# Attention step of a hybrid encoder: the transposes of a block ahead of the scores of a later one, and another rate for the convolution taps

## The chip, the cores and the metric

The kernel runs on one core of a Trainium2 chip, in one launch. The metric is device time in microseconds (us), the median of several runs. The core's engines are TensorE (PE for its matmuls, PEld for its weight loads), VectorE (DVE), ScalarE (ACT), GpSimd (POOL) and SyncE (SP), which here only issues DMAs.

## The reference

One layer of a streaming encoder on a prompt of 1024 frames and 32 frames of a running stream, with 16 heads of 64 and a model width of 1024. Everything starts from one combined projection of the normalised input.

```python
h = rmsnorm(x, norm_g)
cols = lambda a, w: h @ w_in[:, a:a + w]
q = rmsnorm(cols(OFF_Q, ...).reshape(B, T, N_HEADS, HEAD_DIM), q_g) * (HEAD_DIM ** -0.5)
k = rmsnorm(cols(OFF_K, ...), k_g); v = cols(OFF_V, ...)
logf = jax.nn.log_sigmoid(cols(OFF_F, N_HEADS) + b_f)
u = cols(OFF_UA, CONV_WIDTH) * jax.nn.sigmoid(cols(OFF_UB, CONV_WIDTH))
...
s = jnp.einsum('bqhd,bkhd->bhqk', q, k)
s = jnp.where(mask, s + (cq - ck), -inf)          # c = cumsum(logf)
o = jnp.einsum('bhqk,bkhd->bqhd', jax.nn.softmax(s), v)
conv = causal_dwconv(u_ext, w_dw, b_dw)           # 31 taps for each channel
...
ya = (o * jax.nn.silu(ga)) @ w_pa
yb = (jax.nn.silu(layernorm(conv, ln_g, ln_b)) * jax.nn.silu(gb)) @ w_pb
m = jax.nn.sigmoid(ma) * ya + jax.nn.sigmoid(mb) * yb
return x + m @ w_out
```

Two parts of it meet in the change: the causal attention of the prompt, and the depthwise convolution with the LayerNorm over its channels.

## The kernel before, in words

The kernel works with channels on the partitions and frames along the free dimension, and goes through the projections (up to 566 us), the attention (566 to 1045 us) and the output projections. A product in full precision is made of three products of rounded parts (wh, wl for the weight, xh, xl for the input), which line 183 issues. Within a stretch marked as manually scheduled, PE, DVE and ACT, and in the attention SP too, take their instructions in the order in which the program lists them. POOL's order is the scheduler's. An engine does one instruction after another, so one that waits holds up all that is listed behind it.

**The attention.** The list `seq` has, for each of the 16 heads, eight `Block`s (128 queries each, block i with (i + 1) x 128 keys) and in four places a `Sample`, which handles four heads of the running stream: 132 items. The loop at L1244 goes through it, and its step n deals with several items in different stages of their work:

- `scores` (L1110) of item n + 3, through `start`: two matmuls (L1121, L1122) for each bank of up to 512 keys into a psS tile; then on DVE the causal mask is added (L1124) and the maximum taken (L1126).
- `turn` (L1141) of item n: POOL clears a strip (L1146); PE transposes P block by block (L1153) into tiles of psT, which has two banks. The first four transposed blocks are copied out by ACT, the rest (blocks 4 to 7 of a head have some) by DVE (both L1156).
- `soft` (L1129) of item n + 3: the exponential on ACT (L1133), with the sum of each row.
- `norm` (L1136) of item n + 2: the reciprocal on DVE (L1138), the product of P with it on POOL (L1139).
- `fill`, four beats in two halves: a beat is one eighth of a third of a further projection (gates, three matmuls at L183); their results leave through ACT (L944) to DRAM.
- `values` (L1158) of item n - 2, for the last block of a head: 40 matmuls (L1172) into two psT tiles, their copy by ACT (L1176) and sum by DVE (L1177), and for an odd head the product with a gate (L1179) that a DMA brought (L1161).
- one piece of the LayerNorm over channels (L1206 to L1230), once the sums that it needs are there. Its first four pieces are empty; then come six with two matmuls each (L1202), then twelve with small operations of ACT and DVE.

In the first three blocks of head 8 `fill` does nothing (L1258).

**What rides on the beats.** `beat` (L199) counts time in the program's order. It issues the pieces of weight preparation that are due (`prep`: square and maximum, then wh on ACT at L138, wl on DVE at L141), the delayed pieces (`late`), and the convolution's taps. A tap (L371) is one DVE operation over 1086 columns with two tensors read. Taps wait in a list and are dealt by a credit: every beat adds `pace["rate"]`, and while the credit is not negative, the next item is issued and its price taken off, 1 for a tap and 0.1 for the first tap of a channel block, which runs on ACT (L368).

```python
if taps or chores:
    pace["credit"] += pace["rate"]
while pace["credit"] >= 0 and (taps or chores):
    ...
        cost = taps.pop(0)() or 1.0
    pace["credit"] -= cost
```

The rate in the attention is `R_A` (L34, set at L999). Behind the taps of a channel block come its sums (L334, L339); the last block's sums, nine and thirteen beats later (L355, L351), make the LayerNorm ready.

Of the kernel before, what the change touches and what calls it, by code (L numbers as in the profile page):

```python
# [30 lines left out]
LNO = ((0,), (1, 2), (3,), (4, 5), (6,), (7,), ())  # L31
LNEXP = "natural_log_exp_and_others"
NFILL = 22
R_U, R_V, R_QK, R_G, R_A = 0.21, 0.18, 0.165, 0.23, 0.2  # L34
NWARM = 34
HT = TT // 2
HC = HT // 2
# [16 lines left out]
def build(tc, xT, xt, wv, wf, ckT, cv, clT, stT, vec, cst, yT, kT, vO, lfO, cpT, csT):  # L54
# [968 lines left out]
    def fill(n):  # L1023
        for _ in range(n):
            next(flow, None)
# [163 lines left out]
    def start(b):  # L1189
        if getattr(b, "i", 1) == 0:  # L1190
            h = b.head
            if h.h % 2 == 0:
                h.ot = heads[h.h + 1].ot = ap.tile([128, T], F32, name="ot", tag="ot", bufs=2)
        b.scores()

    def pending(b):
        return isinstance(b, Sample) or b.i % 2
# [40 lines left out]
    for n in range(3):  # L1238
# [3 lines left out]
            seq[n - 1].norm()  # L1242
        fill((8, 4, 0)[n])
    for n, b in enumerate(seq):  # L1244
        if n + 3 < len(seq):
            start(seq[n + 3])
        if n + 9 < len(seq) and getattr(seq[n + 9], "i", 1) == 0:
            seq[n + 9].head.load()
        if n + 6 < len(seq) and isinstance(seq[n + 6], Sample):
            seq[n + 6].load()  # L1250
        if getattr(b, "i", 0) == 3 and b.head.h + 1 < H:
            heads[b.head.h + 1].load_v()
        b.turn()
        if n + 3 < len(seq):
            seq[n + 3].soft()
        if n + 2 < len(seq):
            seq[n + 2].norm()
        some = 2 if isinstance(b, Sample) or b.i > 2 or b.head.h != 8 else 0  # L1258
        fill(some)
        if n >= 2 and pending(seq[n - 2]):  # L1260
            seq[n - 2].values()
        fill(some)
        if n >= 3 and isinstance(seq[n - 3], Sample):
            seq[n - 3].finish()
        if "ready" in sides:
            next(ln, None)
# [402 lines left out]
```

## Time and profile before

| | us |
|---|---|
| median of three runs | 1346.9 (1346.65 to 1347.09) |
| the profiled execution | 1345.89 |
| its span, first to last instruction | 1344.1 |
| the attention within it | 566 to 1045 |
| PE busy / DVE busy over the span | 1312.6 / 990.4 |

The profile shows one execution. Times are microseconds from the span's first instruction; a row of a group of instructions gives line, engine, operation, what it writes and reads, count, then the busy time, the mean in ns, and the idle time of the engine just ahead of them with what ended it. In a row of waits, "PE ptr L1153 <- DVE pt L1156: 7.8, 8, 1.7" says that PE's instruction of line 1153 waited for DVE's of line 1156 for 7.8 us in eight places, 1.7 at most. A row of the timeline gives start, duration, engine, line, operation, and in brackets the engine's idle time before it. The ends of matmuls are modelled, and those that follow each other closely overlap.

### The profile page before, as it was taken

What the parts mean: (1) busy time and instruction counts of PE and PEld (TensorE: products, weight loads), DVE (VectorE), ACT (ScalarE), POOL (GpSimd) and SP (SyncE); (2) the same over time, 40 slices, a digit from 0 to 9 for tenths busy, and PEclk for the clock granted to TensorE, in tenths of its full rate; (3) what the DMA queues carried; (4) which work ended last, traced back from release to release, by engine and by line L of the source; (5) the groups of instructions that cost most, each with busy time, mean ns of one, the idle gap of its engine ahead of it and who ended that gap; (6) DMA issues with size and microseconds to landing.
All of it is one profiled execution on the core that took longest, in us unless ns stands there. A gap on an engine that the chain in (4) does not pass through costs nothing.

```text
span 1344.1 us, 24837 instructions
## 1 busy us (share of the span) xinstructions
PE 1312.6 (98%) x9383; PEld 1003.1 (75%) x9383; DVE 990.4 (74%) x1532; ACT 719.0 (53%) x1362; POOL 505.8 (38%) x548
## 2 busy tenths in 40 slices
PE   8999999999999999999889998999999999999999
PEld 5687876666666666667567766777776699999998
DVE  6797879888999997987778866655554489166664
ACT  6644555757676743455555555655555566233320
POOL 2001124547484820243433442222222158255562
PEclk8999999999999999999999999999999999999999
DMA  6343233425352463535644643565452698544462
GB/s 251 98 140 104 93 112 118 139 82 187 95 180 87 162 166 109 160 90 155 165 109 123 186 132 99 147 179 132 131 152 54 240 313 262 176 128 146 142 190 69
DMA packets 113496, 194.97 MB, mean 145 GB/s; under 512 B 34080, under 2 KB 80032, under 8 KB 113376
## 3 DMA queue, kind: packets, MB, share of 16 engines
q1 hardware_dynamic: 113232, 193.31, 46.9%
q8 instruction: 74, 1.21, 0.4%
q14 instruction: 46, 0.38, 0.1%
q10 hardware_dynamic: 144, 0.07, 0.0%
HBM read 127.68 MB, written 65.64 MB: 144 GB/s over the span
## 4 chain that ended last, share of the span: by engine, by line
PE 82%; DVE 9%; ACT 3%; issue 2%; DMA 2%; SPq 1%; POOL 0%; DVEq 0%; ACTq 0%; POOLq 0%
PE pj L183 56%; PE pjv L761 6%; PE pj L1501 6%; PE po L1172 4%; PE ptr L1153 3%; DVE nm L1126 2%; DVE wl L141 2%; DVE y L371 2%; PE psS L1122 2%; PE psS L1121 2%; DMA ga<-s_ga 2%; ACT wh L138 1%; DVE psS L1124 1%; DMA s_q<-qh 1%; PE warm L477 1%
## 5 line engine op out<-in xcount | busy, mean ns | idle before, releaser
L183 PE MATMUL pj<-xh,wh 128*128 128x352 f16 (+2 forms) x1536 | 481.6, 314 | 2.3 <-ACT wh L138 1.4
L183 PE MATMUL pj<-xh,wl 128*128 128x352 f16 (+2 forms) x1536 | 481.2, 313 | 0.7 <-DVE wl L141 0.6
L183 PE MATMUL pj<-xl,wh 128*128 128x352 f16 (+2 forms) x1536 | 480.9, 313 | 0.5 <-DVE xl L579 0.4
L183 PEld LDWEIGHTS <-wh 128*128 128x128 f16 x3072 | 301.5, 98 | 162.1 <-issue 7.1
L371 DVE SCALAR_TENSOR_TENSOR y<-u,vec_t,y 128x1086 f32<-128x1086 f32 x240 | 346.8, 1446 | 12.0 <-ACT y L368 8.9
L1139 POOL TENSOR_SCALAR P<-P,nm 128x128 f32<-128x128 f32 (+7 forms) x128 | 129.9, 1015 | 279.9 <-DVE nm L1138 229.8
L183 PEld LDWEIGHTS <-wl 128*128 128x128 f16 x1536 | 150.5, 98 | 72.0 <-DVE wl L141 1.6
L141 DVE SCALAR_TENSOR_TENSOR wl<-raw,sc,wh 128x384 f16<-128x384 f32 (+1 forms) x192 | 128.2, 693 | 48.3 <-ACT wh L138 48.3
L1133 ACT ACTIVATE P<-psS,nm 128x128 f32<-128x128 f32 (+7 forms) x128 | 95.1, 743 | 113.3 <-DVE nm L1138 70.9
L1126 DVE TENSOR_REDUCE nm<-psS 128x1 f32<-128x128 f32 (+7 forms) x128 | 97.0, 758 | 12.5
L1153 PE MATMUL ptr<-ident,P 128*128 128x128 f32 x576 | 88.6, 276 | 17.3 <-DVE pt L1156 9.2
L175 POOL TENSOR_TENSOR wl<-raw,wh 128x384 fp32r<-128x384 f32 (+1 forms) x51 | 63.3, 1270 | 74.3 <-ACT wh L172 58.6
L1153 PEld LDWEIGHTS ptr<-ident,P 128*128 128x128 f32 x576 | 69.2, 141 | 28.2 <-DVE pt L1156 12.1
L1156 ACT COPY pt<-ptr 128x512 f32<-128x512 f32 (+3 forms) x128 | 64.3, 502 | 44.4 <-PE ptr L1153 43.2
L1121 PE MATMUL psS<-KB,QB 128*128 128x256 f32 (+2 forms) x192 | 81.8, 427 | 0.6 <-ACT P L1133 0.6
L880 POOL TENSOR_TENSOR sql<-sqf,sqh 128x352 fp32r<-128x352 f32 x48 | 57.0, 1187 | 65.8 <-ACT sqh L877 65.8
L138 ACT ACTIVATE wh<-raw,sc 128x1024 f16<-128x1024 f32 (+1 forms) x68 | 73.9, 1091 | 8.2 <-DVE sc L158 7.9
L1172 PE MATMUL po<-pt,V 128*64 128x256 f32 x640 | 72.8, 382 | 2.5 <-ACT pts L1078 1.7
L1124 DVE TENSOR_TENSOR psS<-psS,cmask 128x128 f32<-128x128 f32 x128 | 37.6, 294 | 46.0 <-PE psS L1122 45.6
L906 POOL TENSOR_TENSOR ql<-qn,qh 128x352 fp32r<-128x352 f32 (+1 forms) x48 | 67.8, 1429 | 6.6 <-ACT qh L905 6.5
L761 PE MATMUL pjv<-vwh,xh 128*128 128x260 f16 x256 | 70.1, 274 | 0.0
L761 PE MATMUL pjv<-vwl,xh 128*128 128x260 f16 x256 | 70.0, 273 | 0.0
(271 smaller groups left out, 2532.9 us busy)
## 6 DMA issues: line engine op xcount, KB each, us to landing
raw<-wf SPq DMA_DIRECT2D x92, 512.0 KB
QB<-s_q SPq DMA_DIRECT2D x32, 256.0 KB
KB<-s_k SPq DMA_DIRECT2D x32, 256.0 KB
kT<-qn SPq DMA_DIRECT2D x8, 528.0 KB
s_ga<-t SPq DMA_DIRECT2D x24, 176.0 KB
s_gb<-t SPq DMA_DIRECT2D x24, 176.0 KB
s_ma<-t SPq DMA_DIRECT2D x24, 176.0 KB
s_mb<-t SPq DMA_DIRECT2D x24, 176.0 KB
```

Source lines behind the costliest of these rows:

```text
L138: nc.scalar.mul(wh[:, ks, :], raw[:, ks, :], self.s[:, i:i + 1])
L141: nc.vector.scalar_tensor_tensor(wl[:, ks, :], raw[:, ks, :], self.s[:, i:i + 1], wh[:, ks, :], op0=ALU.mult, op1=ALU.subtract)
L183: nc.tensor.matmul(ps, a[:, kt, :], b(kt, sl), start=(first and n == 0), stop=(last and n == N - 1))
L371: t = nc.vector.scalar_tensor_tensor(y, u[:, i:i + CW], w, y, op0=ALU.mult, op1=ALU.add)
L761: nc.tensor.matmul(ps[:, :VC], a, b, start=(n == 0), stop=(n == 23))
L1121: nc.tensor.matmul(ps[:, b, :wm], QB[:, qsl], KB[:, ksl], start=True, stop=False)
L1126: nc.vector.tensor_reduce(nm[:, 0:1], ps[:, :nb, :w], axis=AX.XY, op=ALU.max, negate=True)
L1133: nc.scalar.activation(P[:, :nk].rearrange("p (b w) -> p b w", b=nb), ps[:, :nb, :w], AF.Exp, bias=nm[:, 0:1], accum_out=nm[:, 1:2])
L1139: nc.gpsimd.tensor_scalar(P[:, :nk], P[:, :nk], nm[:, 2:3], 1.0, op0=ALU.mult, op1=ALU.mult)
L1153: nc.tensor.transpose(pt[:, 128 * j:128 * j + 128], P[:, 128 * (4 * u + j):128 * (4 * u + j) + 128], ident)
L1172: nc.tensor.matmul(po[rows], V[:, j, :], parts[c][:, j, :], start=(c % 2 == 0 and j < 2), stop=(c % 2 == 1 and j >= 2 * c))
L1501: nc.tensor.matmul(pss[c][:, :HC], a[:, k, :], x, start=(not more and kt == 0 and n == 0), stop=(kt == 3 and n == 2), skip_group_check=more)
```

## The change

```diff
-R_U, R_V, R_QK, R_G, R_A = 0.21, 0.18, 0.165, 0.23, 0.2
+R_U, R_V, R_QK, R_G, R_A = 0.21, 0.18, 0.165, 0.23, 0.165
...
     for n, b in enumerate(seq):
+        b.turn()
         if n + 3 < len(seq):
             start(seq[n + 3])
         if n + 9 < len(seq) and getattr(seq[n + 9], "i", 1) == 0:
             seq[n + 9].head.load()
         if n + 6 < len(seq) and isinstance(seq[n + 6], Sample):
             seq[n + 6].load()
         if getattr(b, "i", 0) == 3 and b.head.h + 1 < H:
             heads[b.head.h + 1].load_v()
-        b.turn()
         if n + 3 < len(seq):
             seq[n + 3].soft()
```

The first edit sets the credit that a beat of the attention adds from 0.2 to 0.165, so about six beats pass from tap to tap where five did. The second lists the transposes of item n, their copies and the clearing of a strip ahead of the scores of item n + 3, their mask and maximum, and ahead of the loads of a later head. The instructions themselves stay the same.

## The prediction

> **What bounds the kernel now.** The page comes first: the span, and the busy time of each engine.
>
> ```profile
> span 1344.1 us, 24837 instructions
> PE 1312.6 (98%) x9383; PEld 1003.1 (75%) x9383; DVE 990.4 (74%) x1532; ACT 719.0 (53%) x1362; POOL 505.8 (38%) x548
> ```
>
> PE is the bound, so the change can only win idle PE time or lose more of it. The profiled execution took 1345.89 us, 1.8 us of it outside the span; the median of the runs is 1346.9, 1.0 above. I work on the profiled execution and put the difference on the median.
>
> The attention runs from 566 to 1045 us. The table of windows (PE, PEld, DVE, ACT, POOL, clock, DMA) splits it where the conv taps end and the LayerNorm's sums begin (809), and where head 8 ends (844).
>
> ```profile
> 566.00:809.00 243.00, 229.41 (x1705) 165.70 (x1704) 185.75 (x358) 136.73 (x294) 95.59 (x111) 1.00 0.49 134
> 809.00:844.00 35.00, 30.33 (x191) 21.66 (x191) 23.14 (x56) 18.78 (x44) 7.34 (x13) 0.95 0.46 118
> 844.00:1045.00 201.00, 198.13 (x1503) 143.94 (x1502) 112.98 (x281) 117.31 (x255) 51.60 (x94) 1.00 0.48 130
> ```
>
> PE is idle for 243.0 - 229.4 = 13.6 us in the first stage, 4.7 in the second, 2.9 in the third: 21.2 us is all that can be won. DVE is 76% busy in the first stage and 56% in the third. Who waits for whom (us, times, longest), in the first stage and then in the third:
>
> ```profile
> DVE wl L141 <- ACT wh L138: 11.2, 8, 2.2
> DVE psS L1124 <- PE psS L1122: 11.5, 17, 2.3
> PE ptr L1153 <- DVE pt L1156: 7.8, 8, 1.7
> PE ptr L1153 <- ACT pt L1156: 3.2, 3, 1.1
> ```
>
> ```profile
> DVE psS L1124 <- PE psS L1122: 32.1, 29, 2.1
> PE ptr L1153 <- DVE pt L1156: 1.4, 3, 0.6
> ```
>
> The masking add (L1124) waits for its scores in only 17 of 66 blocks of the first stage; in the other 49 DVE comes to it late. The result is PE's largest wait: a transpose needs a PSUM bank (psT has two) that DVE has not yet copied out (L1156). The timeline shows one such wait whole.
>
> ```profile
> 586.33 0.40 PE L1121 MATMUL psS<-KB,QB 128*128 128x256 f32 x1
> 586.69 0.82 PE L1153 MATMUL ptr<-ident,P 128*128 128x128 f32 x6
> 587.48 1.14 ACT L138 ACTIVATE wh<-raw,sc 128x1024 f16<-128x1024 f32 x1
> 588.64 0.62 DVE L141 SCALAR_TENSOR_TENSOR wl<-raw,sc,wh 128x384 f16<-128x384 f32 x1 [2.12 <-ACT wh L138]
> 589.18 1.34 DVE L371 SCALAR_TENSOR_TENSOR y<-u,vec_t,y 128x1086 f32<-128x1086 f32 x1
> 590.97 0.29 DVE L1124 TENSOR_TENSOR psS<-psS,cmask 128x128 f32<-128x128 f32 x1
> 591.37 0.29 DVE L1126 TENSOR_REDUCE nm<-psS 128x1 f32<-128x128 f32 x1
> 591.57 0.41 DVE L1156 COPY pt<-ptr 128x256 f32<-128x256 f32 x1
> 592.04 0.55 PE L1153 MATMUL ptr<-ident,P 128*128 128x128 f32 x3 [1.74 <-DVE pt L1156]
> ```
>
> DVE stands 2.12 us before a weight split because ACT makes its input only after an exponential, then runs a tap, then add and maximum of the block three ahead, and only then the copy that PE needs.
>
> **Part one, the thinner taps.** No instruction is added or removed; taps move later.
>
> ```profile
> L371 DVE SCALAR_TENSOR_TENSOR y<-u,vec_t,y 128x1086 f32<-128x1086 f32 x46 | 64.0, 1391 | 2.3 <-ACT y L368 2.2
> ```
>
> 46 taps at a price of 1, four sums at 1 and a first tap at 0.1 are 50.1 units. The last starts after 49.1 units: beat 246 at 0.2, 298 at 0.165; the last sum is ready 13 beats later, at 259 and 311. With 12 beats ahead of the loop, 4 a step and none in head 8's first three steps, that is about step 60, and step 77 after the change. By beat 256 the new rate has dealt 42.2 units, 7.9 fewer: 7.9 x 1.391 = 11.0 us of DVE time leave the first stage. At most the share in which DVE is late turns into PE time, 49 of 66, or 8.2 us; at least nothing, since lag that a later idle moment absorbs costs PE nothing. PE's waits for the copy are 7.8 us, so I take half: **-4.1 us**. The taps land in heads 8 and 9, where the cover is the 32.1 us that DVE spends waiting for scores in the third stage; were it gone, the 11.0 us would come back as lag.
>
> A second effect is in POOL's normalisation (L1139), by width, first stage and then third:
>
> ```profile
> L1139 POOL TENSOR_SCALAR P<-P,nm 128x1024 f32<-128x1024 f32 x8 | 12.0, 1502 | 8.2 <-ACT P L1133 4.5 <-DVE nm L1138 3.5
> L1139 POOL TENSOR_SCALAR P<-P,nm 128x128 f32<-128x128 f32 x9 | 8.5, 944 | 26.2 <-DVE nm L1138 22.4 <-ACT P L1133 3.3 <-DVE sc L157 0.4
> ```
>
> ```profile
> L1139 POOL TENSOR_SCALAR P<-P,nm 128x1024 f32<-128x1024 f32 x7 | 7.9, 1135 | 6.2 <-DVE nm L1138 6.1
> L1139 POOL TENSOR_SCALAR P<-P,nm 128x128 f32<-128x128 f32 x6 | 2.3, 388 | 13.3 <-DVE nm L1138 8.8 <-ACT P L1133 4.4
> ```
>
> The same operation takes 1502 against 1135 ns, 944 against 388, where taps run beside it. [...] I price it at nothing: POOL idles before each norm.
>
> **Part two, the turn ahead of the scores.** A step issues on PE turn(n), then scores(n+3); on DVE copy(n), then add and maximum of n+3. ACT's order does not change (the scores have no ACT work). The turn of a Block issues no DMA; that of a Sample issues one, but in none of the four Sample steps does a load stand ahead of it, so nothing is passed on SP. POOL's memset passes nothing either.
>
> Gain: the copy comes before add and maximum. In the timeline that is 591.57 - 590.97 = 0.60 us; after a block of 1024 it is about 1.5:
>
> ```profile
> L1126 DVE TENSOR_REDUCE nm<-psS 128x1 f32<-128x1024 f32 x16 | 19.6, 1224 | 1.7
> L1124 DVE TENSOR_TENSOR psS<-psS,cmask 128x128 f32<-128x128 f32 x128 | 37.6, 294 | 46.0 <-PE psS L1122 45.6
> ```
>
> Losses: the scores no longer stand ahead of a blocked transpose. They take 586.69 - 586.33 = 0.36 us for the narrowest block, up to about 1. And a copy that used to fit into DVE's wait for wh now stands ahead of add, maximum, exponential and wh, so that chain ends 0.2 us later and more. In the example 0.60 - 0.2 - 0.36 is about 0. Behind the maximum wait, on ACT, the exponential and all that follows it; behind the transposes, on PE, scores and projection. The whole attention's PE waits:
>
> ```profile
> PE ptr L1153 <- DVE pt L1156: 9.2, 11, 1.7
> PE ptr L1153 <- ACT pt L1156: 6.4, 5, 2.2
> ```
>
> Eleven waits for DVE gain 0 to 1.5 us less 0.36; I take 0.3 each, -3.3. Five waits for ACT do not end earlier and lose cover of 0.36 to 1: 0.6 each, +3.0. Sum -0.3; ends: -9.2 (all DVE waits gone) and +9.6 (none ends earlier, 16 x 0.6). A turn also reaches its norm earlier by one block of scores; POOL held PE's weight load for 1.8 us in the first stage, three times:
>
> ```profile
> PEld ptr L1153 <- POOL P L1139: 1.8, 3, 1.2
> ```
>
> I take +0.3 for it, so part two is **0**.
>
> **Head 8.** Its first three steps have no projection to fill PE; the LayerNorm's sums run there now and will run from step 81, in filled steps.
>
> ```profile
> L1202 PE MATMUL psn<-rstd,ones_f 128*128 128x352 f32 x6 | 2.5, 494 | 0.6 <-ACT pt L1156 0.6
> L1202 PE MATMUL psn<-mean,ones_f 128*128 128x352 f32 x6 | 2.4, 476 | 0.0
> ```
>
> ```profile
> DVE ot L1179 <- DMA ga<-s_ga: 2.9, 1, 2.9
> PE ptr L1153 <- ACT pt L1156: 2.2, 1, 2.2
> PE ptr L1153 <- DVE ot L1177: 1.2, 1, 1.2
> ```
>
> DVE waits 2.9 us for the gate's DMA and PE then 1.2 us for DVE. The DMA's landing stays, so about half of the 4.9 us of sums becomes idle: +2.4. The 2.2 us wait for ACT, whose queue carried the LayerNorm's pieces, goes: -2.2. I take **0**, ends -4 and +4.2. The upper one has another half-clock stretch in it: the clock of 0.95 over 35 us is 1.75 us now.
>
> [...]
>
> **Sum**: -4.1 + 0 + 0 = -4.1: 1341.8 for the profiled execution, 1342.8 for the median.
>
> **Rivals.** (1) *No change*: the lag that fewer taps save is absorbed where DVE idles anyway, and wh, not the taps, sets each wait. For it: the episode begins with the 2.12 us wait for wh. Against: DVE late in 49 of 66 blocks. Part one gives 0 to -1: about 1346. (2) *Slower: transposes blocked with nothing in front.* The waits end when they end now, and each leaves its scores undone. Price 0.6 x 16 = 9.6 us at worst; with half to all of it, part one at -2 to 0 and head 8 at +2: 1346.9 + 5 to 11, 1352 to 1358, likeliest 1352. It decides once some eight of the sixteen waits end no earlier. For it: the chain through wh gets longer. Against: at a 1024-wide maximum the copy gains 1.5 us. (3) *Both parts work in full*: part one -8, most of the copy waits gone: about 1335.
>
> **How the numbers follow.** Forecast (1340 to 1344.1) 0.38; rival 3 and what lies between 0.12; rival 1 0.22; rival 2 0.28. A measurement of this kernel can tell about 0.2%, 2.7 us, from no change. Faster 0.50, same 0.22, slower 0.28. The range, 1335.5 to 1352, leaves out the far ends of rivals 2 and 3.
>
> **What would show it.** Right: about 38 taps before the LayerNorm's first sum, which stands in head 9's last step; PE's wait for the DVE copy below 5 us over the attention; PE idle in heads 0 to 7 near 9.5. Part two wrong: waits of the transposes for ACT or POOL above 8 us. Head 8 wrong: idle over 6 us around the gate's DMA, clock below 0.95. The whole is wrong if DVE's add is still late in three blocks of four.

## The result and the profile after

The changed kernel took 1360.4 us in the median of four runs (1358.3 to 1361.2), the kernel before 1347.0 beside it. The ratio is 1.0077, with a 95% interval of 1.0059 to 1.0095: slower by some 10 us. The profiled execution took 1358.31 us.

The first rows of the page after:

```profile
span 1356.5 us, 24807 instructions
...
PE 1318.2 (97%) x9383; PEld 992.5 (73%) x9383; DVE 987.9 (73%) x1532; ACT 714.7 (53%) x1362; POOL 512.4 (38%) x548
```

The span is 12.4 us longer. The table of windows for the stages of the prediction (PE, PEld, DVE, ACT, POOL, clock, DMA):

```profile
566.00:809.00 243.00, 230.99 (x1708) 160.35 (x1707) 179.49 (x352) 132.38 (x290) 95.76 (x108) 1.00 0.48 132
809.00:844.00 35.00, 30.35 (x198) 20.34 (x197) 23.76 (x53) 17.84 (x40) 11.23 (x14) 0.95 0.58 147
844.00:1045.00 201.00, 193.06 (x1429) 133.49 (x1427) 109.77 (x274) 111.16 (x249) 51.18 (x92) 0.98 0.46 126
```

DVE has 6.3 us less to do in the first stage (179.49 against 185.75), and PE's idle time falls there from 13.6 to 12.0 us. In the third stage it rises from 2.9 to 7.9 us, and the clock falls from 1.00 to 0.98. PE's waits over the whole attention after the change:

```profile
PE ptr L1153 <- ACT pt L1156: 11.3, 8, 3.1
PE ptr L1153 <- POOL P L1139: 5.9, 5, 2.6
PE ptr L1153 <- DVE os_t L1102: 3.0, 2, 2.3
...
PE ptr L1153 <- DVE pt L1156: 1.6, 2, 1.1
```

The waits for the DVE copy, at which the edit is aimed, are nearly gone: 9.2 us before, 1.6 now. In their place stand waits for the ACT copy (6.4 before) and for POOL's norm. ACT's own waits point to a reason; before, then after:

```profile
ACT P L1133 <- DVE nm L1138: 70.9, 62, 3.1
ACT pt L1156 <- PE ptr L1153: 43.2, 50, 2.1
ACT P L1133 <- DVE nm L1126: 38.4, 30, 3.3
```

```profile
ACT P L1133 <- DVE nm L1138: 162.3, 103, 4.2
...
ACT pt L1156 <- PE ptr L1153: 8.8, 11, 1.8
```

(By the program all that the exponential needs of DVE is the maximum of its own block, L1126. The reciprocal that stands behind it on DVE, L1138, is the block before's; in the block shown below it ends 0.07 us after the maximum, and the row names it.) ACT's exponential waited 109 us for DVE before and 162 after.

**One block in both traces.** Block 4 of head 3, whose fifth transpose needs a second bank. Before:

```profile
675.50 0.48 PE L1121 MATMUL psS<-KB,QB 128*128 128x448 f32 x1
...
676.98 1.09 DVE L1126 TENSOR_REDUCE nm<-psS 128x1 f32<-128x896 f32 x1
...
678.17 1.01 ACT L1133 ACTIVATE P<-psS,nm 128x896 f32<-128x896 f32 x1 [0.50 <-DVE nm L1138]
...
678.70 0.47 PE L1121 MATMUL psS<-KB,QB 128*128 128x512 f32 x1
...
679.16 1.14 ACT L138 ACTIVATE wh<-raw,sc 128x1024 f16<-128x1024 f32 x1
...
679.71 0.60 PE L1153 MATMUL ptr<-ident,P 128*128 128x128 f32 x4
680.21 0.54 ACT L944 ACTIVATE t<-pj,sc 128x352 f32<-128x352 f32 x1
...
680.73 0.58 ACT L1156 COPY pt<-ptr 128x512 f32<-128x512 f32 x1
...
681.37 0.33 PE L1153 MATMUL ptr<-ident,P 128*128 128x128 f32 x1 [1.05 <-ACT pt L1156]
```

After:

```profile
676.64 0.45 PE L1121 MATMUL psS<-KB,QB 128*128 128x448 f32 x1
...
678.08 1.09 DVE L1126 TENSOR_REDUCE nm<-psS 128x1 f32<-128x896 f32 x1
...
679.29 1.01 ACT L1133 ACTIVATE P<-psS,nm 128x896 f32<-128x896 f32 x1 [1.78 <-DVE nm L1138]
...
679.46 0.60 PE L1153 MATMUL ptr<-ident,P 128*128 128x128 f32 x4
...
680.29 1.14 ACT L138 ACTIVATE wh<-raw,sc 128x1024 f16<-128x1024 f32 x1
681.32 0.54 ACT L944 ACTIVATE t<-pj,sc 128x352 f32<-128x352 f32 x1
...
681.85 0.58 ACT L1156 COPY pt<-ptr 128x512 f32<-128x512 f32 x1
...
682.49 0.33 PE L1153 MATMUL ptr<-ident,P 128*128 128x128 f32 x1 [2.43 <-ACT pt L1156]
```

Follow the chain from a step's first score to the fifth transpose of the next step: scores, maximum, exponential, weight split, evacuation (and a small copy of a Sample, 0.2 us), copy of the first four transposes, free bank. It takes 681.37 - 675.50 = 5.87 us before and 682.49 - 676.64 = 5.85 after. PE's own way between the two points became shorter. Before, it still had that step's turn to do, and at the next step the scores (678.70 to 679.71) ahead of the transposes. After, it has neither: from the first score to the end of the four transposes it is 4.81 us before (to 680.31) and 3.42 after (to 680.06). So the same chain is waited for 2.43 us instead of 1.05.

**The sum of the loss.** At the last sums of head 15 the changed kernel is 12.7 us behind. PE's idle time in the attention is 5.9 us larger (27.0 against 21.1, over 494.80 us and 482.10). Two more stretches at a clock of 0.50 lie in it, three (their rows stand in the last section) against one (825.5 to 828.9 us in the kernel before), each about 3.4 us long, so about 1.7 us lost in each: 3.4. (The rate alone, below, has as many by its clock, 1.00 up to 806 us, 0.96 over 806 to 845 and 0.98 over 845 to 1045: at 1.7 us a stretch that is about one and two. So the profile doesn't put these to the order.) The remaining 3.4 us are counted as busy time of PE, and no row names them.

### The profile page after: what moved, and what is told of

It is laid out like the page before. It is cut to its first block, busy times and chain, and to the rows that moved or that the text cites. A ratio compares the mean times of both kernels' runs of the same rounds, so it can differ in the third digit from the quotient of the medians.

```text
span 1356.5 us, 24807 instructions
## 1 busy us (share of the span) xinstructions
PE 1318.2 (97%) x9383; PEld 992.5 (73%) x9383; DVE 987.9 (73%) x1532; ACT 714.7 (53%) x1362; POOL 512.4 (38%) x548
## 4 chain that ended last, share of the span: by engine, by line
PE 83%; DVE 7%; ACT 4%; issue 3%; DMA 1%; POOL 1%; SPq 0%; DVEq 0%; ACTq 0%; POOLq 0%
PE pj L183 56%; PE pjv L761 6%; PE pj L1501 6%; PE po L1172 5%; PE ptr L1153 3%; PE psS L1122 2%; PE psS L1121 2%; DVE nm L1126 2%; DVE wl L141 1%; ACT wh L138 1%; DVE y L371 1%; ACT P L1133 1%; DVE psS L1124 1%; DMA ga<-s_ga 1%; PE pst L860 1%
## 5 line engine op out<-in xcount | busy, mean ns | idle before, releaser
L1139 POOL TENSOR_SCALAR P<-P,nm 128x128 f32<-128x128 f32 (+7 forms) x128 | 135.8, 1061 | 285.7 <-DVE nm L1138 263.7
L1133 ACT ACTIVATE P<-psS,nm 128x128 f32<-128x128 f32 (+7 forms) x128 | 95.1, 743 | 168.6 <-DVE nm L1138 162.3
L1153 PE MATMUL ptr<-ident,P 128*128 128x128 f32 x576 | 88.5, 276 | 23.8 <-ACT pt L1156 11.3
L1126 DVE TENSOR_REDUCE nm<-psS 128x1 f32<-128x128 f32 (+7 forms) x128 | 97.0, 758 | 12.5
L1121 PE MATMUL psS<-KB,QB 128*128 128x256 f32 (+2 forms) x192 | 76.9, 402 | 0.0
L120 POOL CAST topb<-tops 128x2 bf16<-128x2 f32 x35 | 18.4, 527 | 136.5 <-ACT junk L117 86.6
L761 PE MATMUL pjv<-vwh,xl 128*128 128x260 f16 x256 | 69.9, 273 | 0.0
```

What stands on the lines that cost most here:

```text
L761: nc.tensor.matmul(ps[:, :VC], a, b, start=(n == 0), stop=(n == 23))
L1121: nc.tensor.matmul(ps[:, b, :wm], QB[:, qsl], KB[:, ksl], start=True, stop=False)
L1126: nc.vector.tensor_reduce(nm[:, 0:1], ps[:, :nb, :w], axis=AX.XY, op=ALU.max, negate=True)
L1133: nc.scalar.activation(P[:, :nk].rearrange("p (b w) -> p b w", b=nb), ps[:, :nb, :w], AF.Exp, bias=nm[:, 0:1], accum_out=nm[:, 1:2])
L1139: nc.gpsimd.tensor_scalar(P[:, :nk], P[:, :nk], nm[:, 2:3], 1.0, op0=ALU.mult, op1=ALU.mult)
L1153: nc.tensor.transpose(pt[:, 128 * j:128 * j + 128], P[:, 128 * (4 * u + j):128 * (4 * u + j) + 128], ident)
```

## The experiments

Three sets of four kernels, each compared with the kernel before in its own set, whose median stood at 1351.4 to 1351.6 us there. So ratios are compared, also between sets, and a difference in us is the ratio's on 1347.0.

**Which of the two parts?** Theory A: the order. Theory B: the rate, by which the LayerNorm's sums come to lie in filled steps. Theory C: only both together.

The order alone:

```diff
-R_U, R_V, R_QK, R_G, R_A = 0.21, 0.18, 0.165, 0.23, 0.165
+R_U, R_V, R_QK, R_G, R_A = 0.21, 0.18, 0.165, 0.23, 0.2
```

> Part two alone (turn ahead of the scores, rate 0.2 as before). Theory A (the order: with no scores in front of them the transposes wait for POOL's norm and ACT's copies, and the waits show as bubbles): 1355 to 1360 us, PE's waits for POOL and for ACT about 17 us in the attention. Theory B (the rate: LayerNorm's sums and its ACT and DVE pieces land in filled heads 10 and 11): 1343 to 1348, with no stall over 2.5 us behind the taps. Theory C (both are needed): 1346 to 1350.

Measured 1365.3 us, ratio 1.0110 (1.0079 to 1.0141): **+14.8 us**. PE's waits there:

```profile
PE ptr L1153 <- ACT pt L1156: 15.8, 11, 4.4
PE ptr L1153 <- DVE pt L1156: 6.2, 4, 3.6
PE ptr L1153 <- POOL P L1139: 2.5, 4, 1.4
```

The waits for ACT and POOL are 18.3 us, as theory A had it; the time, 1361.8 us by the ratio, is 2 us above its range. PE's idle time over the attention is 34.1 us here, 13 more than in the kernel before. The waits for the DVE copy are still 6.2 us, so the fall to 1.6 in the changed kernel is not the order's alone. The rate alone, with the scores ahead of the turn as before:

```diff
-        b.turn()
         if n + 3 < len(seq):
             start(seq[n + 3])
...
+        b.turn()
         if n + 3 < len(seq):
             seq[n + 3].soft()
```

> Part one alone (rate 0.165, scores still ahead of the turn). Theory A: 1343 to 1347 us. Theory B: 1354 to 1360, with LayerNorm's sums in heads 9 and 10 and long waits of the transposes for ACT there, and about two half-clock stretches more than before. Theory C: 1345 to 1350.

Measured 1346.2 us, ratio 0.9965 (0.9953 to 0.9977): **-4.7 us**. The two parts alone add up to +10.1, the whole change measured +10.4. B and C fall: nothing is left over for a joint effect. One sign of B did come, two half-clock stretches more than before. The waits for the DVE copy over the attention, and the third stage of that execution, the slowest of its ten at 1348.98 us:

```profile
PE ptr L1153 <- DVE pt L1156: 8.8, 9, 1.9
```

```profile
844.00:1045.00 201.00, 194.25 (x1435) 140.22 (x1432) 114.60 (x284) 114.64 (x251) 50.70 (x89) 0.98 0.44 120
```

PE is idle there for 6.8 us at a clock of 0.98, almost as in the changed kernel (7.9 and 0.98). So the worse third stage doesn't tell the slow kernel from the fast one either.

The next two move the three steps without projection to the head where the LayerNorm's sums now lie, first in the changed kernel, then with the rate alone:

```diff
-        some = 2 if isinstance(b, Sample) or b.i > 2 or b.head.h != 8 else 0
+        some = 2 if isinstance(b, Sample) or b.i > 2 or b.head.h != 10 else 0
```

> The changed kernel with the three steps without fill moved from head 8 to head 10, so that LayerNorm's sums again fall on the steps that they fell on before. Theory A: within 2 us of the changed kernel, 1357 to 1361. Theory B: most of the 13 us comes back, 1345 to 1350. Theory C: 1347 to 1354, as the places where the two meet move but don't go.

> Part one alone with the steps without fill moved to head 10. Theory A: as part one alone, 1343 to 1347 us. Theory B: 8 us or more below part one alone, 1344 to 1348. Theory C: 1343 to 1348, within 2 us of part one alone.

Measured 1.0077 (1.0054 to 1.0100) and 0.9957 (0.9942 to 0.9972). Neither differs from its partner (1.0077 and 0.9965) by more than its interval. Where the sums lie makes no difference that these runs can tell.

**What in the order?** Theory A1: the scores come later, so the exponential does, and on ACT's queue it holds up what stands behind it. Theory A2: PE stands at its transposes because nothing is in front of them, whenever the exponential comes. The scores four blocks ahead, still behind the turn, take away A1's cause and leave A2's:

```diff
         fill((8, 4, 0)[n])
+    start(seq[3])
...
-        if n + 3 < len(seq):
-            start(seq[n + 3])
+        if n + 4 < len(seq):
+            start(seq[n + 4])
```

> The changed kernel with the scores asked four blocks ahead instead of three, still behind the turn, so that the exponential of a step finds its maximum done. Theory A1 (the later scores make the exponential late, and on ACT's queue it holds up the evacuations and the next copy of the transposes): the loss goes, 1340 to 1346 us, and ACT's wait for DVE's reciprocal and maximum ahead of the exponential falls from 162 us to under 30. Theory A2 (PE stands at its transposes because nothing is in front of them, whenever the exponential comes): 1354 to 1361 us, PE's waits for ACT's copy and for POOL as in the changed kernel, 17 us.

Measured 1337.7 us, ratio 0.9904 (0.9884 to 0.9923): **-12.9 us**, 23 us below the changed kernel by one edit, and faster than A1 had it. The waits of PE, then of ACT:

```profile
PE ptr L1153 <- POOL P L1139: 7.3, 7, 2.7
PE ptr L1153 <- ACT pt L1156: 3.0, 4, 1.0
```

```profile
ACT P L1133 <- DVE nm L1138: 6.9, 6, 3.8
```

The exponential finds its maximum done: 6.9 us instead of 162.3. In the block shown above, it starts 0.49 us after the copy does, and the fifth transpose waits 0.68 us:

```profile
675.98 0.59 ACT L1156 COPY pt<-ptr 128x512 f32<-128x512 f32 x1 [1.20 <-PE ptr L1153]
...
676.47 1.01 ACT L1133 ACTIVATE P<-psS,nm 128x896 f32<-128x896 f32 x1
...
679.92 0.33 PE L1153 MATMUL ptr<-ident,P 128*128 128x128 f32 x1 [0.68 <-ACT pt L1156]
```

Its partner has the same edit with the scores ahead of the turn:

> Part one alone (rate 0.165, scores ahead of the turn) with the scores asked four blocks ahead: the partner of the run before, with the same free exponential and the other order on PE. A1: within 2 us of it, 1340 to 1345. A2: 10 us or more below it. Against both: the scores at a step's start now need the bank that the exponential of the step before leaves, and if that is late, PE waits for ACT's exponential (psS), which could cost up to 3 us.

Measured 1340.5 us, ratio 0.9925 (0.9906 to 0.9944). With a free exponential, the order on PE makes no difference that these intervals can separate (-2.8 us, give or take 3.7). A2 falls as a cause of its own: within these limits PE's order costs something only while the exponential is late. The drawback named in advance is there: PE's scores wait 4.1 us for the exponential to leave their bank. Even so the kernel is 5.4 us (give or take 3.0) below the rate alone, which suggests that the late exponential cost something in the old order too.

Two runs put the scores back in front of the second bank's transposes. In the first only blocks with one bank turn first; in the second the turn is cut in two.

```diff
-        b.turn()
+        first = getattr(b, "i", 7) < 4
+        if first:
+            b.turn()
...
+        if not first:
+            b.turn()
```

> The changed kernel, but only the blocks with one bank of transposes (i under 4) turn first; the blocks with two banks ask for the scores first, as before. A1: about half of the loss stays, 1348 to 1353 us, as every late exponential counts. A2 by the second bank (PE reaches the second bank's transposes before ACT has copied the first of its two banks): nearly all of the loss goes, 1342 to 1346.

```diff
-        b.turn()
+        if isinstance(b, Block):
+            b.turn((0,))
         if n + 3 < len(seq):
             start(seq[n + 3])
...
+        if isinstance(b, Block):
+            b.turn((1,))
+        else:
+            b.turn()
```

> The changed kernel with the turn cut in two: the first four transposes, then the scores three blocks ahead, then the other transposes and DVE's copy. A1: the exponential is nearly as late as in the changed kernel, 1350 to 1358 us. A2 by the second bank: the scores again stand between the two banks, 1340 to 1346 us.

Measured 0.9989 (0.9980 to 0.9999) and 1.0005 (0.9993 to 1.0016), or 3.2 and 5.4 us above the rate alone, where the full turn is 15.1 above. On 1347.0 these are 1345.5 and 1347.7 us, so neither expectation fits both runs: most of the loss goes, as A2 by the second bank had it, and about a fifth and a third stay. So most of the loss lies with the blocks that have two banks. That fits the chain above, in which the distance from the scores to the second bank's transposes counts and the scores of the next block are a part of it.

The last test of the chain leaves the order on PE and DVE as in the changed kernel and moves the exponential on ACT alone:

```diff
-        if n + 3 < len(seq):
-            seq[n + 3].soft()
...
         fill(some)
+        if n + 3 < len(seq):
+            seq[n + 3].soft()
         if n >= 2 and pending(seq[n - 2]):
```

> The changed kernel with one move: the exponential of the block three ahead is issued behind the step's first two pieces of filling product instead of ahead of them, so that on ACT's queue it no longer stands, waiting for its maximum, in front of the weight split and the evacuation. A1 (the wait at the head of ACT's queue is the loss): most of the 15 us comes back, 1342 to 1350 us by the clean clock of the first runs, ACT's wait for DVE's reciprocal falls from 162 us to under 60. A2 (the order on PE itself): within 3 us of the changed kernel. Against A1: the exponential and the norm behind it come later for PE's transposes, two steps on; if that bites, PE waits for POOL's norm more than 6 us.

Measured 1349.3 us, ratio 0.9980 (0.9965 to 0.9995): 2.0 us above the rate alone (give or take 2.6) instead of 15.1. So **13 of the 15 us** come back. The same block, from the first score to the fifth transpose:

```profile
674.47 0.45 PE L1121 MATMUL psS<-KB,QB 128*128 128x448 f32 x1
...
675.23 1.15 ACT L138 ACTIVATE wh<-raw,sc 128x1024 f16<-128x1024 f32 x1
...
677.11 1.01 ACT L1133 ACTIVATE P<-psS,nm 128x896 f32<-128x896 f32 x1 [0.72 <-DVE nm L1138]
...
679.27 0.33 PE L1153 MATMUL ptr<-ident,P 128*128 128x128 f32 x1 [1.39 <-ACT pt L1156]
```

The weight split now runs while the maximum is made. The chain takes 679.27 - 674.47 = 4.80 us instead of 5.85, and the wait at its end falls by as much, from 2.43 to 1.39 us. Over the attention PE's waits for the ACT copy fall only from 11.3 to 7.5 us and those for POOL from 5.9 to 4.6; what else makes up the 13 us was not traced. One number of the expectation was wrong: ACT's wait ahead of the exponential fell only to 145.0 us, not below 60.

```profile
ACT P L1133 <- DVE nm L1138: 145.0, 100, 5.2
```

So most of that wait cost nothing by itself. It costs where work that PE needs stands behind it.

**What is left of the rate, and is there a better kernel?** The kernel with the scores four ahead behind the turn, once at the old rate, once with the free steps in head 10, once with thinner taps (`R_A` 0.2; `b.head.h != 10`; `R_A` 0.14):

> The scores four ahead behind the turn, with the taps at the old rate of 0.2. If the thinner taps act alone (worth 0.35% with the scores ahead of the turn), this stands 3 to 6 us above the same kernel at rate 0.165. If the free exponential already hides what DVE was late with, the two are within 2 us.

> The scores four ahead behind the turn at rate 0.165, with the three steps without fill moved to head 10, where LayerNorm's sums now fall. If the sums in filled steps still cost what they seemed to cost in the changed kernel (heads 10 and 11 lost 9 us there), 3 to 8 us less than with the steps in head 8; if those losses were the same late exponentials, within 2 us.

> The scores four ahead behind the turn with the taps thinner still, rate 0.14. If DVE's load in the stage of the taps is still what PE waits for, 1 to 4 us less than at 0.165. If nothing of it is left there (PE waits 0.3 us for DVE's copies at 0.165), within 2 us, or slower where LayerNorm's later steps run past the attention's end.

Measured 0.9898 (0.9869 to 0.9928), 0.9890 (0.9861 to 0.9920) and 0.9873 (0.9841 to 0.9905), in medians 1338.5, 1337.6 and 1334.3 us, beside 0.9904 at 0.165. The differences are smaller than the intervals, so no ranking follows. Between the rates of 0.2 and 0.165 no gain of the thinner taps is seen any more, but 4 us could hide in the noise. All of them beat both kernels, by 13 to 17 us against the kernel before.

## Why the prediction was wrong

- **Part one, -4.1: right in size, its working not borne out.** Measured alone, -4.7 (-6.3 to -3.1). The first stage lost 6.3 us of DVE time in the changed kernel and 0.9 with the rate alone, not 11.0, and the sign of "about 38 taps" failed: 44 of the 46 start in that stage (the first row, of the changed kernel's line 371), since the stage runs on some steps past the beat for which the prediction counted. Nor does DVE come to its add in time more often: it waits for the scores in 17 of 66 blocks of the stage, as before (the second row), and in 20 of 67 with the rate alone. That is still late in about three blocks of four, which the prediction set as a sign that the whole is wrong.

```profile
L371 DVE SCALAR_TENSOR_TENSOR y<-u,vec_t,y x44: 1330/1332/2217, 566.0 to 805.8; 128x1086 f32<-128x1086 f32 x44
```

```profile
DVE psS L1124 <- PE psS L1122: 12.5, 17, 1.7
```

  With the rate alone PE's waits for the DVE copy, of which half was to go, are 8.8 us over the attention instead of 9.2. PE's idle time in the first stage is 10.5 us there instead of 13.6, but the third stage gives that back. So the half that was taken as gain hit the size by luck, and where the 4.7 us come from stays open. With the exponential free the gain is no longer seen, within the limits above; late taps may also have been paid through the late maximum, but that was not tested.
- **Head 8, 0: right within the measurement.** Moving the free steps under the sums changed neither kernel by more than its interval, and the clock in that stage is 0.95 again. The two halves of the term, +2.4 and -2.2, were not measured apart. The sums began at 866.3 us, in the step of head 9's block 6, one step before the text had them.
- **Part two, 0 with ends at -9.2 and +9.6: this step failed.** It measured +14.8 (10.6 to 19.0), beyond its own upper end. The prediction priced the sixteen waits that were in the trace, "Five waits for ACT do not end earlier and lose cover of 0.36 to 1: 0.6 each". But the lost cover also makes waits where the ACT copy had come in time: with the order alone there are eleven of them instead of five, and 15.8 us instead of 6.4. It also named the thing itself, "Behind the maximum wait, on ACT, the exponential and all that follows it", and gave it no price. The block above shows that price: the chain of 5.87 us stayed, PE's way to its end became 1.4 us shorter, and the wait rose by as much, where the sum allowed 0.36 to 1. The gain was smaller than the waits suggest: those for the DVE copy fell from 9.2 to 6.2 us by the order alone, and to 1.6 only with both parts. In the changed kernel ACT and POOL took their place with 17.2 us, over the 8 us set as the sign that part two is wrong.
- **Rival 2** had the right mechanism, transposes blocked with nothing in front of them, with too low a price for the same reason: at worst 0.6 x 16. It lacked the second half: the missing cover costs only while the exponential stands late at the head of ACT's queue. With the exponential free the same order is no slower, as far as the intervals tell.
- That work on ACT's queue waits behind an exponential that stands there shows in the block above: after the wait of 1.78 us weight split, evacuation and copy start one behind the other (680.29, 681.32 and 681.85 us), and moving that one instruction on the queue gave 13 us back.

The prediction's range ended at 1352 us. The added half-clock stretches (3.4 us) appear in none of part two's terms; the rate alone shows as many.

## What to carry to other kernels

A move on one engine changes the distance between the start of a chain and the place where its result is needed: take the chain's length from the timeline, and subtract the time that the waiting engine fills between the two points, before and after, for every repetition and not just for those that already wait. If an in-order queue has a long wait at its head, ask what stands behind it and who needs that; here an earlier start of the waited-for work (scores one block sooner) was worth 23 us, and a reordering of the queue 13. A wait total alone is no cost: with 145 us of ACT's waiting the kernel was 2 us above the rate alone, with 162 us 15.

## What the runs showed of the hardware

Three stretches of the changed kernel's attention, each about 3.4 us long, show a clock of 0.50. Just before each, PE stood idle for 2.33 to 3.13 us in one piece; the longest of these idles ends 0.2 us into its stretch. The three transposes that ended them, with the idle time before each:

```profile
815.65 0.44 PE L1153 MATMUL ptr<-ident,P 128*128 128x128 f32 x2 [2.65 <-POOL P L1139]
```

```profile
928.52 0.33 PE L1153 MATMUL ptr<-ident,P 128*128 128x128 f32 x1 [2.33 <-DVE os_t L1102]
```

```profile
892.67 0.47 PE L1153 MATMUL ptr<-ident,P 128*128 128x128 f32 x1 [3.13 <-ACT pt L1156]
```

The table of windows of the stretches (clock third from the end):

```profile
892.50:895.90 3.40, 3.23 (x10) 1.95 (x11) 1.99 (x6) 0.12 (x1) 0.00 (x0) 0.50 0.75 253
930.00:933.40 3.40, 3.40 (x14) 2.09 (x13) 3.12 (x7) 1.57 (x3) 1.01 (x1) 0.50 0.01 2
817.40:820.80 3.40, 3.40 (x20) 1.94 (x18) 1.31 (x3) 1.55 (x4) 1.57 (x4) 0.50 1.04 216
```

Each of these stretches cost about 1.7 us by the clock. Not each such idle brings one: the block shown from head 3 waited 2.43 us, and the clock was 1.00 from 679.8 to 687.7 us. And in the kernel before, the one such stretch of the attention came behind shorter idles, of 1.25 and 0.57 us:

```profile
823.48 0.52 PE L1153 MATMUL ptr<-ident,P 128*128 128x128 f32 x3 [1.25 <-DVE ot L1177]
824.57 0.86 PE L1202 MATMUL psn<-rstd,ones_f 128*128 128x352 f32 x2 [0.57 <-ACT pt L1156]
```

```profile
825.50:828.90 3.40, 3.40 (x14) 2.37 (x13) 1.86 (x5) 1.85 (x4) 0.80 (x1) 0.50 0.67 159
```

So in these traces the length of one idle does not tell by itself whether half clock follows. What does is not shown here.
